# Stick-breaking projections of two heads at a time by seven block products, with the split sets of x stored and reloaded

## The chip, the cores and the metric

The kernel runs on one core of one Trainium2 chip. Its time is device microseconds for one launch. The kernel before takes 2082.61 us, the median of two runs (2079.24 and 2085.99).

The engines are called as the profile calls them: PE is TensorE (matmuls; PEld are its weight loads), DVE is VectorE, ACT is ScalarE, POOL is GpSimd, and SP is the engine that issues nearly all transfers of this kernel.

## The reference

One decoder layer on 1024 tokens of width 2048, in float32:

```python
h = rmsnorm(x, g_pre)
u = h @ w_in                       # 2048 -> 7184 columns, split among the groups
gq, gk, gv, g_gate, g_lr, sq, sk, sv, s_gate = split(u)
log_a = log_sigmoid(g_lr @ w_a2 + b_a) / 16
o_gla = rmsnorm(gla_chunked(gq, gk, gv, log_a), g_gla_head) * silu(g_gate)   # 4 heads
o_sb  = stick_breaking(sq, sk, sv) * silu(s_gate)                            # 8 heads of 128
#   z = q k^T / sqrt(128);  A[t,s] = sigmoid(z_ts) * prod_{s<j<t} (1 - sigmoid(z_tj))
x = x + rmsnorm(concat(o_gla, o_sb) @ w_out, g_post)
x = x + sigmoid(x @ w_g + b_g) * (p @ w_p)
```

## The kernel before, in words

All activations stand transposed: 128 channels in the partitions, tokens along the row. A token half `hf` has 512 tokens. PE multiplies a pair of 128-channel blocks at a time into a PSUM tile of 512 tokens (`dn`, four buffers). To keep float32 precision each operand is split into a rounded high part and the rest, by `split` (lines 112 to 114: a copy on ACT, a subtraction on DVE), and each product is three matmuls: high by high, low by high, high by low (`hi`/`lo` or `wh`/`wl` are weights, `ah`/`al` activations).

**The units.** `dense` (line 144) makes one unit: 128 output columns for both halves, over all 16 channel blocks. It loads the weights in four blocks of 256 KB (`wload`, line 123: two `raw` buffers, four `hi`, four `lo`), and each block feeds 4 channel blocks x 2 halves x 3 matmuls. There are 16 units for GLA (k, q and two of v for each of 4 heads) and 24 for stick-breaking (k, q, v for each of 8 heads). The result is scaled by `rstd`, the norm of x, on its way out of PSUM (`evac_plain`, `evac_turned`, lines 311 to 329); v is turned by a transposing transfer (`turn_by_dma`, line 331: ACT, SP) and copied together by DVE.

**Attention beside the units.** `gla` (line 352) and `sb` (line 541) are generators in the queue `jobs`. After every channel block of a unit `step` (line 174) advances them by `rate[1]` steps, 1.0 for GLA and 0.9 for stick-breaking, and every `pace[1]` steps the queue `beside`. In `sb` a head takes 38 steps: its k is split, then for each of 6 items `scores` (line 580) makes z on PE, two sigmoids on ACT, masks on POOL (memset, affine select), a scan and a product on DVE, and a transposing transfer. After L1 = 8 steps `turned` (line 611) copies the result together on DVE (line 618) and splits it, and after L2 = 8 more `values` multiplies it by the turned v. The queries' factor 1/sqrt(128) is a constant scale of the sigmoids (lines 592 and 593).

**The gate.** The 16 blocks of gate columns come from seven block products per block row (a Strassen-Winograd scheme over 2 x 2 blocks: two halves of channels, two halves of tokens, two halves of columns). `x_sums` (line 690) makes four sums of x's blocks (S1 to S4) on ACT and DVE beside the units, one k in 60 steps, and stores them unsplit. Sixteen of the products are small ones under the last of the attention (`small_product`, line 778: two blocks of 256 KB), the other 40 are wide (`product`, line 899: 512 KB weights, `wr`, `wh`, `wl`). Sums of weights are made by DVE (`add`, `sub`, lines 881 and 884) and stored for later products (`g2_d`, `g3_d`); sets of x are loaded from their stored sums and split again (`x_set`, `fill`).

The output projection and the last gate follow with the same scheme; the change leaves them alone.

**What sets the order.** A planner orders each engine's instructions ahead of the run, by its own costs and by priority: program order, moved ahead by `tc.high_priority(offset=...)`. Each engine then works strictly in that order, and waits where an operand is not there. Buffers of a tag are reused in turn, so a load can wait for the last reader of its buffer.

POOL issues one transfer in the whole kernel (line 108), SP and ACT the others. The scratch of POOL's transfers is set in line 1379:

```python
nc = bacc.Bacc("TRN2", target_bir_lowering=False, num_devices=1,
               dynamic_dma_scratch_size=512)
```

## Time and profile before

| | before |
|---|---|
| median of two runs | 2082.61 us (2079.24 to 2085.99) |
| span of the profiled execution | 2075.1 us |
| PE busy | 2060.6 us (99%), 9712 matmuls |
| PEld busy | 1706.3 us (82%) |
| DVE busy | 1481.9 us (71%) |
| ACT busy | 874.1 us (42%) |
| POOL busy | 112.0 us (5%) |
| moved by DMA | 352.81 MB, mean 170 GB/s |
| granted clock of PE | 1.000 |

The profile is one execution, which has a page and a trace. The page gives its span, from the first to the last instruction, and no other time of that execution; the runs' times include what lies around the span. A group's row reads: line, engine, operation, output<-inputs by the program's names, shape, count | busy us, mean ns of one | idle us of the engine just before them, and what ended it. A row of windows reads: stretch, its length, then for each engine busy us and number of instructions, the granted clock, the mean busy share of the 16 DMA engines, GB/s. A row of waits reads: who <- for whom: us in total, times, longest. A row of transfers has the size and the median us from issue to landing. A matmul's duration overlaps with the next one's, so their means do not add up to time.

### The profile page before, as it was taken

What the parts mean: (1) busy time and instruction counts of PE and PEld (TensorE: products, weight loads), DVE (VectorE), ACT (ScalarE), POOL (GpSimd) and SP (SyncE); (2) the same over time, 40 slices, a digit from 0 to 9 for tenths busy, and PEclk for the clock granted to TensorE, in tenths of its full rate; (3) what the DMA queues carried; (4) which work ended last, traced back from release to release, by engine and by line L of the source; (5) the groups of instructions that cost most, each with busy time, mean ns of one, the idle gap of its engine ahead of it and who ended that gap; (6) DMA issues with size and microseconds to landing.
All of it is one profiled execution on the core that took longest, in us unless ns stands there. A gap on an engine that the chain in (4) does not pass through costs nothing.

```text
span 2075.1 us, 26732 instructions
## 1 busy us (share of the span) xinstructions
PE 2060.6 (99%) x9712; PEld 1706.3 (82%) x9712; DVE 1481.9 (71%) x2243; ACT 874.1 (42%) x1390; POOL 112.0 (5%) x229
## 2 busy tenths in 40 slices
PE   9999999999999999999999999999999999999998
PEld 6788888888888888888888788888888888888887
DVE  8657777676766676666567677788778687886765
ACT  7333334333454554555447423344233334423322
POOL 4100000000011011101001000000000000000000
PEclk9999999999999999999999999999999999999999
DMA  6222222232243344443326798888978486886752
GB/s 219 69 67 78 82 78 82 66 87 67 62 126 88 106 107 108 113 105 97 84 79 156 213 328 295 306 298 303 335 283 269 163 313 229 307 292 210 243 190 98
DMA packets 229700, 352.81 MB, mean 170 GB/s; under 512 B 124336, under 2 KB 129344, under 8 KB 229568
## 3 DMA queue, kind: packets, MB, share of 16 engines
q1 hardware_dynamic: 228960, 349.00, 53.2%
q10 hardware_dynamic: 576, 2.10, 0.3%
q8 instruction: 76, 1.25, 0.2%
q14 instruction: 56, 0.46, 0.1%
q0 software_dynamic: 32, 0.01, 0.0%
HBM read 249.85 MB, written 73.92 MB: 156 GB/s over the span
## 4 chain that ended last, share of the span: by engine, by line
PE 90%; DVE 3%; DMA 3%; issue 2%; ACT 1%; SPq 0%; POOL 0%; DVEq 0%; ACTq 0%; POOLq 0%
PE dn L101 79%; PE z L101 5%; PE t L101 3%; PE o L101 3%; DMA E<-X 1%; DMA xraw<-xT 1%; DVE rstd L235 0%; DMA u<-xT 0%; DVE lo L114 0%; DVE al L252 0%; DVE X L603 0%; DVE E L608 0%; DMA raw<-w_gate 0%; ACT hi L113 0%; ACT ah L251 0%
## 5 line engine op out<-in xcount | busy, mean ns | idle before, releaser
L101 PE MATMUL dn<-ah,hi 128*128 128x512 f32 x1408 | 561.7, 399 | 2.3 <-ACT u L736 1.9
L101 PE MATMUL dn<-ah,lo 128*128 128x512 f32 x1408 | 549.6, 390 | 0.2 <-DVE lo L114 0.2
L101 PE MATMUL dn<-al,hi 128*128 128x512 f32 x1408 | 549.4, 390 | 0.0
L101 PE MATMUL dn<-ah,wl 128*128 128x512 f32 x1216 | 473.4, 389 | 0.0
L101 PE MATMUL dn<-al,wh 128*128 128x512 f32 x1216 | 473.1, 389 | 0.0
L101 PE MATMUL dn<-ah,wh 128*128 128x512 f32 x1216 | 473.1, 389 | 0.0
L101 PEld LDWEIGHTS dn<-ah,hi 128*128 128x128 f32 x1408 | 265.0, 188 | 60.2 <-issue 3.6
L101 PEld LDWEIGHTS dn<-al,hi 128*128 128x128 f32 x1408 | 264.3, 188 | 57.6 <-DVE al L252 0.4
L101 PEld LDWEIGHTS dn<-ah,lo 128*128 128x128 f32 x1408 | 265.2, 188 | 48.1 <-DVE lo L114 0.5
L113 ACT ACTIVATE wh<-wr 128x1024 fp32r<-128x1024 f32 x152 | 159.4, 1055 | 268.1 <-PE dn L101 168.9
L101 PEld LDWEIGHTS dn<-ah,wl 128*128 128x128 f32 x1216 | 228.3, 188 | 48.7 <-DVE wl L114 1.2
L101 PEld LDWEIGHTS dn<-al,wh 128*128 128x128 f32 x1216 | 228.3, 188 | 47.3
L101 PEld LDWEIGHTS dn<-ah,wh 128*128 128x128 f32 x1216 | 228.3, 188 | 47.3
L114 DVE TENSOR_TENSOR wl<-wr,wh 128x1024 fp32r<-128x1024 f32 x152 | 185.0, 1218 | 7.0 <-ACT wh L113 6.7
L113 ACT ACTIVATE hi<-raw 128x512 fp32r<-128x512 f32 x192 | 119.7, 625 | 153.4 <-PE dn L101 137.9
L114 DVE TENSOR_TENSOR lo<-raw,hi 128x512 fp32r<-128x512 f32 x192 | 134.7, 703 | 59.6 <-ACT hi L113 59.5
L333 ACT ACTIVATE X<-E 128x256 uint16<-128x256 uint16 (+2 forms) x96 | 81.0, 844 | 142.8 <-DVE E L608 70.2
L603 DVE TENSOR_TENSOR_SCAN X<-X 128x128 f32<-128x128 f32 (+2 forms) x96 | 97.8, 1019 | 14.4 <-POOL X L597 13.0
L618 DVE COPY v<-E 128x512 uint16<-128x512 uint16 (+1 forms) x160 | 64.1, 430 | 48.5 <-DMA E<-X 45.3
L114 DVE TENSOR_TENSOR s<-v,s 128x512 fp32r<-128x512 f32 (+1 forms) x82 | 52.6, 642 | 61.1 <-ACT s L113 60.9
L884 DVE TENSOR_TENSOR wr<-wr,wr 128x1024 f32<-128x1024 f32 x48 | 58.7, 1223 | 49.4 <-issue 15.1
L881 DVE TENSOR_TENSOR wr<-wr,wr 128x1024 f32<-128x1024 f32 x48 | 58.7, 1224 | 47.5 <-DMA wr<-w_g 34.0
(246 smaller groups left out, 2292.6 us busy)
## 6 DMA issues: line engine op xcount, KB each, us to landing
raw<-w_in SPq DMA_DIRECT2D x160, 256.0 KB, 2.7
wr<-w_g SPq DMA_DIRECT2D x64, 512.0 KB, 4.4
wr<-w_out SPq DMA_DIRECT2D x56, 512.0 KB, 4.8
wr<-w_gate SPq DMA_DIRECT2D x40, 512.0 KB, 5.2
g_d<-wr SPq DMA_DIRECT2D x32, 512.0 KB, 3.8
wr<-g_d SPq DMA_DIRECT2D x32, 512.0 KB, 4.5
ar<-h_d SPq DMA_DIRECT2D x28, 512.0 KB, 4.9
ar<-og_d SPq DMA_DIRECT2D x25, 512.0 KB, 5.3
```

The source lines that it names most:

```text
L101: PE.matmul(o, lhsT, rhs, start=start, stop=stop)
L113: A.activation(hi, src, AF.Copy)
L114: (eng or V).tensor_tensor(lo, src, f(hi), op=ALU.subtract)
L333: A.activation(pl.rearrange("p (two n) -> p two n", two=2), src.bitcast(U16)[:, :2 * n].rearrange("p (n two) -> p two n", two=2), AF.Copy)
L603: V.tensor_tensor_scan(rev, rev, rev, initial=kq[:, n:n + 1], op0=ALU.mult, op1=ALU.bypass)
L618: V.tensor_copy(to[:, :, :m, j], w[:, :, 2 * g:2 * g + m])
L881: V.tensor_tensor(dst, a, b, op=ALU.add)
L884: V.tensor_tensor(dst, a, b, op=ALU.subtract)
```

## The change

**Pairs of heads.** The 24 stick-breaking units become 12 pairs of units: for two heads k beside q of each, and the two v. A pair is a block matrix of 2 (halves of channels) x 2 (columns) by 2 (token halves), made by the seven products that the gate already used, each over 8 channel blocks: 24 matmuls for one token half's sum. `by_waves` makes four of the seven (with the sets A11, s1, S2, A22), `by_stages` three (A12, S4, S3). The pairs go three at a time through first and second passes: pairs 0 to 5 first waves, then stages, pairs 6 to 11 first stages, then waves.

**Sets of x.** `x_sets` replaces `x_sums`: it runs in the GLA units (one k in 25 steps), splits its four sums at once, and stores high and low parts, as also those of the plain blocks A11, A12 and A22. Four sets of 8 high and 8 low tiles are resident at a time; `swap` and `load_set` reload a set over one that is done with, 8 transfers of 512 KB, without splitting again. 8 sets are reloaded in the stick-breaking products and 3 in the gate's. The last GLA unit (`dense_by_blocks`) goes by blocks of 12 matmuls, so that two sets are free early.

**Sums of weights.** Within a chain the next product's weights are the last ones plus another block. `extend` adds that block to the tile in place by a transfer that accumulates, issued by POOL. `onto` does the same with results: a first pass writes k, q and v (unscaled) to DRAM, the second accumulates onto them there.

**The attention** fetches k, q and v from DRAM as it comes to a head (`fetch`, `take`), scales k and v by `rstd` on DVE, and turns v then; q's scale goes into the sigmoids as a column per token (`rq`, made by eight transposes on PE in `norm_first`). It starts when two heads are complete, after 33 of the 84 products, and runs at a rate of 1.0. Half of the copies in `turned` go to ACT (`regroup`).

**The gate** has 32 small products (in batches of 3, 3 and 2 by `by_waves`) and 24 wide ones. The weights' sums on DVE and their storing fall to one addition per column block.

The diff, cut to its core:

```diff
+def pair_offsets():
+    offs = []
+    for h in range(0, SB_HEADS, 2):
+        offs += [(OFF_SK + P * h, OFF_SQ + P * h), (OFF_SK + P * h + P, OFF_SQ + P * h + P),
+                 (OFF_SV + P * h, OFF_SV + P * h + P)]
     return offs
...
-RATE_SB = 0.9
+RATE_SB = 1.0
...
+Q1, V0, V1, NEXT_Q, NEXT_K = 8, 3, 14, 30, 33
...
-LAST_11 = 4
-PACE_QKV, PACE_TAIL = 15, 4
+RATE_TAIL = 1.0
+PACE_X, PACE_SET = 5, 2
+ACCUMULATE, REGROUP = True, 1
+BATCHES = ((0, 1, 2), (3, 4, 5), (6, 7))
...
+        def regroup(j, dst, src):
+            if j >= REGROUP:
+                A.activation(dst, src, AF.Copy)
+            else:
+                V.tensor_copy(dst, src)
...
+            def fetch(h, what, hf):
+                if (h, what, hf) not in fetched and h in sb_ready:
+                    fetched[h, what, hf] = t = at("u")
+                    dma2(t, kqv_d[h][what][hf])
+
+            def take(h, what, hf):
+                fetch(h, what, hf)
+                return fetched.pop((h, what, hf))
...
+                    raw = take(h, 0, hf)
+                    kh[hf], kl[hf] = at(tag, dt=F32R), at("u", dt=F32R)
+                    V.tensor_tensor(raw, raw, rstd[hf], op=ALU.mult)
+                    split(kh[hf], kl[hf], raw)
...
+                    def turn_first():
+                        t = take(h, 2, hf)
+                        V.tensor_tensor(t, t, rstd[hf], op=ALU.mult)
+                        vp[hf] = turn_by_dma(t, HT, "u", "u")
+
+                    def turn_last():
+                        full, w = at("u"), vp[hf]
+                        V.tensor_copy(full.bitcast(U16).rearrange("p (c t two) -> p two c t", c=4, two=2), w)
+                        vp[hf] = at("u", dt=F32R), at("u", dt=F32R)
+                        split(*vp[hf], full)
...
-                    A.activation(kq[:, :n], z[:, :n], AF.Sigmoid, scale=-scale)
-                    A.activation(sg[:, :n], z[:, :n], AF.Sigmoid, scale=scale)
+                    for t, r in ((kq, rq[1]), (sg, rq[0])):
+                        A.activation(t[:, :n], z[:, :n], AF.Sigmoid, scale=r[:, 4 * hf + qi:4 * hf + qi + 1])
...
-                            V.tensor_copy(to[:, :, :m, j], w[:, :, 2 * g:2 * g + m])
+                            regroup(j, to[:, :, :m, j], w[:, :, 2 * g:2 * g + m])
...
+            tp = ps("z")
+            for c in range(4):
+                PE.transpose(ch(tp, c), ch(rstd[hf], c), idn)
+            for t, scale in zip(rq, (1.0, -1.0)):
+                V.tensor_scalar(t[:, 4 * hf:4 * hf + 4], tp[:, ::P], scale * float(P) ** -0.5, None, op0=ALU.mult)
...
             def keep(name, k, t):
-                dma2(part(sx_d[name][k // 2], k), t)
-
+                hi, lo = xs.tile([P, HT], F32R, tag="xh", name=nm("xh"), bufs=2), t.bitcast(F32R)
+                split(hi, lo, t)
+                for d, s in zip(sx_d[name][k // 2], (f(hi), t)):
+                    dma2(part(d, k), s)
...
+                A.activation(a21, a21, AF.Copy, scale=g)
+                V.scalar_tensor_tensor(s1, s1, g8, a21, op0=ALU.mult, op1=ALU.subtract)
+                yield 1
+                V.scalar_tensor_tensor(a21, a11, gminus[:, k:k + 1], a21, op0=ALU.mult, op1=ALU.add)
                 keep("S3", k, a21)
...
+                store_plain()
+                yield 1
+                a12 = x_part(0, k + 8)
+                V.scalar_tensor_tensor(a11, a11, gminus[:, k:k + 1], s1, op0=ALU.mult, op1=ALU.subtract)
+                keep("s1", k, s1)
...
+        def load_set(name, slot):
+            got = []
+            for i, (hf, kp) in enumerate(home[slot]):
+                pair = act_wide(hf, kp)
+                for d, t in zip(sx_d[name][i], pair):
+                    with tc.issue_after(last_load[0]):
+                        dma2(f(t), d)
+                    yield 1
+                got.append(pair)
+            sets[name] = parts(got)
+
+        def swap(old, new):
+            sets.pop(old, None)
+            slot = place.pop(old)
+            place[new] = slot
+            beside.append(load_set(new, slot))
...
+            for hf, q in ((1, 0), (1, 1), (0, 2), (0, 3), (0, 0), (0, 1), (1, 2), (1, 3)):
+                hi, lo = wload(wsrc[q])
+                begin, end = q == (0 if hf else 2), q == (3 if hf else 1)
+                for kk in range(4):
+                    ah, al = acts[hf][4 * q + kk]
+                    sl = slice(kk * P, (kk + 1) * P)
+                    mm(out_ps[hf], hi[:, sl], ah, begin and kk == 0, False)
+                    mm(out_ps[hf], lo[:, sl], ah, False, False)
+                    mm(out_ps[hf], hi[:, sl], al, False, end and kk == 3)
+                    if kk % 2:
+                        step()
+                if (hf, q) == (1, 1):
+                    swap("A21", "s1")
+                if (hf, q) == (0, 3):
+                    swap("A12", "S2")
...
+        def begin(i, src):
+            chain[i] = []
             for q in range(2):
...
+                t = wt("ch", 6)
+                last_load[0] = dma(t, part(src, q)).ins
+                chain[i].append(t)
+
+        def extend(i, src):
+            for q, t in enumerate(chain[i]):
+                if ACCUMULATE:
+                    G.dma_start(t, part(src, q), accum_op=ALU.add)
+                    continue
+                raw = wt("raw", 2)
+                last_load[0] = dma(raw, part(src, q)).ins
+                V.tensor_tensor(t, t, raw, op=ALU.add)
...
+                    hi, lo = wt("hi", 4, F32R), wt("lo", 4, F32R)
+                    split(hi, lo, chain[i][q])
...
+        def onto(dst, t, first):
+            if first:
+                dma2(dst, t)
+            else:
+                G.dma_start(dst, t, accum_op=ALU.add)
+
+        def kept(p, scale=1.0):
+            t = wt("pt", 4)
+            A.activation(t, p, AF.Copy, scale=scale)
+            return t
...
+        def by_waves(items, first, weight, at_d, swaps, mid=None):
+            upper, fifth = {}, {}
+            names = ("A11", "s1", "S2", "A22")
+            blocks = ((0, 0), (0, 1), (1, 1), (1, 0))
+            for s, x in sorted(((s, x) for s in range(4) for x in range(len(items))),
+                               key=lambda v: (1, v[1] + 1.5) if v[0] == 2 else v):
+                i = items[x]
+                if mid and (s, x) == (2, 0):
+                    mid()
+                with early():
+                    (begin if s == 0 else extend)(i, weight(i, *blocks[s]))
+                p = ps("dn")
+                small_product(names[s], i, p)
+                if x == len(items) - 1 and names[s] in swaps:
+                    swap(names[s], swaps[names[s]])
+                with soon():
+                    if s == 0:
+                        upper[i] = kept(p)
+                        onto(at_d("c11", i), upper[i], first)
+                    elif s == 1:
+                        fifth[i] = p
+                    else:
+                        V.tensor_tensor(upper[i], p, upper[i], op=ALU.add)
+                    if s == 2:
+                        t = wt("pt", 4)
+                        V.scalar_tensor_tensor(t, fifth[i], -1.0, upper[i], op0=ALU.mult, op1=ALU.subtract)
+                        for m in ("c12", "c22"):
+                            if at_d(m, i) is not None:
+                                onto(at_d(m, i), t, first)
+                    elif s == 3:
+                        onto(at_d("c21", i), upper[i], first)
+
+        def by_stages(items, first, weight, at_d, swaps):
+            for m in ((2, 3, 7) if first else (3, 7, 2)):
+                name = {2: "A12", 3: "S4", 7: "S3"}[m]
+                for i in items:
+                    with early():
+                        if m == 7:
+                            extend(i, weight(i, 0, 1))
+                        else:
+                            begin(i, weight(i, 1, 1 if m == 3 else 0))
+                    p = ps("dn")
+                    small_product(name, i, p)
+                    with soon():
+                        onto(at_d({2: "c11", 3: "c12", 7: "c22"}[m], i), kept(p), first)
+                        if m == 7:
+                            onto(at_d("c21", i), kept(p, -1.0), first)
...
+        to_2, to_1 = {"A11": "S4", "s1": "S3", "S2": "A12"}, {"A12": "A11", "S4": "s1", "S3": "S2"}
+        def sb_items(stage, first, b, swaps={}):
+            stage(range(3 * b, 3 * b + 3), first, lambda i, kh, nh: w_sb[i, kh, nh], sb_d, swaps)
+            pace[1] = PACE_SET
+            if not first:
+                sb_ready.update({2 * b: True, 2 * b + 1: True})
+                rate[1] = RATE_SB
+
+        sb_items(by_waves, True, 0)
+        sb_items(by_waves, True, 1, to_2)
+        sb_items(by_stages, False, 0)
+        sb_items(by_stages, False, 1)
+        sb_items(by_stages, True, 2)
+        sb_items(by_stages, True, 3, to_1)
+        sb_items(by_waves, False, 2)
+        sb_items(by_waves, False, 3)
...
+        def gate_batch(js, swaps={}, mid=None):
+            by_waves(js, True, lambda j, kh, nh: w_gate[kh, nh, j],
+                     lambda m, j: part(g_d[m][j // 2], j) if m in g_d else None, swaps, mid)
+
+        rate[1] = RATE_TAIL
+        for js in BATCHES[:-1]:
+            gate_batch(js)
...
+    gate_batch(BATCHES[-1], {"A11": "A12", "s1": "S3", "S2": "S4"}, to_wide)
...
+                w2_ = wsplit(wload2(w_gate[1, 0, j]))
+                t3, b22 = wload2(w_gate[0, 1, j]), wload2(w_gate[1, 1, j])
+                add(t3, t3, b22)
+                w7, w3 = wsplit(t3), wsplit(b22)
+                if j % 2 == 0:
+                    with tc.issue_after(last_load[0]):
+                        dma2(st_v[j // 2], g_d["c21"][j // 2])
+                        dma2(st_u[j // 2], g_d["c12"][j // 2])
+            if j % 2 == 0:
+                p11 = staged(g_d["c11"][j // 2])
+            p = product(need("A12"), w2_)
+            gate(j, 0, p, part(p11, j), add)
+            if j == 7:
+                job(fill("A11", 0, plain(og_d[0])))
+                rate[1] = 1.0
+            p = product(need("S3"), w7)
+            gate(j, 1, p, v(j), lambda z, p, c: sub(z, c, p))
+            gate(8 + j, 1, p, u(j), add)
+            p = product(need("S4"), w3)
+            gate(8 + j, 0, p, u(j), add)
...
```

More of the change, by code (lines that the diff above doesn't have):

```diff
@@ L211, in layer @@
     pair = {}
+    x_wide = {}
     acc = {}
@@ L662, in layer @@
         sb_ready = {}
+        kqv_d = [[[dram.tile([P, HT], F32, name=f"kqv{h}{i}{hf}_d") for hf in HALVES] for i in range(3)]
+                 for h in range(SB_HEADS)]
         def norm_first(hf):
@@ L782, in small_product @@
+        def small_product(name, i, p):
+            while name not in sets:
+                assert beside
+                advance(beside)
+            a = sets[name]
+            for q in range(2):
+                with tc.high_priority(offset=700):
+                    hi, lo = wt("hi", 4, F32R), wt("lo", 4, F32R)
+                    split(hi, lo, chain[i][q])
                 for kk in range(4):
@@ L808, in keep_11 @@
-        def keep_11(j, new):
-            def go(p):
-                t = new()
-                V.tensor_tensor(t, p, part(u1_s[j // 2], j) if j < 6 else u1_s[j], op=ALU.add)
-                dma2(part(c11_d[j // 2], j), t)
-            return go
-        while beside:
-            advance(beside)
-        rate[1], pace[1] = RATE_TAIL, PACE_TAIL
-        beside.append(x_set("S2", 1))
-        for j in range(8):
-            small_product(x_act[0][:8], w_gate[0, 0, j], keep_u1(j))
-        while beside:
-            advance(beside)
@@ L858, in state @@
         def state(which):
-            return [act.tile([P, W], F32, tag=f"{which}0_{kp}", name=nm("st")) for kp in range(4, 8)]
+            return [act.tile([P, W], F32, tag=f"{which}{hf}_{kp}", name=nm("st")) for hf, kp in home[0]]
         def to_slot(s, i, raw):
@@ L1023, in finish, with need @@
             dma2(og_d[hf][kp], z)
-        def gates_11():
-            for i in range(4):
-                finish(staged(c11_d[i]), 0, i)
-                yield 1
-        t2_d, t3_d = drams("g2_d", 8), drams("g3_d", 8)
-        dma2(st_u[3], u1_d)
+        def need(name):
+            while name not in sets:
+                assert beside
+                advance(beside)
+            return sets[name]
         for j in range(8):
             with ahead():
-                b11, t1, t2 = (wload2(w_gate[kh, nh, j]) for kh, nh in ((0, 0), (0, 1), (1, 1)))
-                sub(t1, t1, b11)
-                sub(t2, t1, t2)
-                w2, w1 = wsplit(t2), wsplit(t1)
-                add(b11, b11, t2)
-                dma2(t2_d[j], t2)
-                dma2(t3_d[j], b11)
-            p = product(g_sets["S2"], w2)
-            with soon():
-                add(u(j), p, part(u1_s[j // 2], j) if j < 6 else u(j))
-            p = product(g_sets["S1"], w1)
-            with soon():
-                add(v(j), p, u(j))
@@ L1048, in layer @@
-        drain()
-        job(fill("S3", 1, plain(sx_d["S3"])))
-        job(fill("S4", 2, plain(sx_d["S4"])))
-        job(gates_11())
-        for j in range(8):
-            with ahead():
-                t4, t2 = wload2(w_gate[1, 0, j]), wload2(t2_d[j])
-                add(t4, t4, t2)
-                w = wsplit(t4)
-            p = product(x_act[1][8:], w)
-            with soon():
-                add(u(j), p, u(j))
-        drain()
-        for j in range(8):
-            with ahead():
-                w = wsplit(wload2(t3_d[j]))
-            p = product(sets["S3"], w)
-            gate(j, 1, p, u(j))
-            gate(8 + j, 1, p, v(j))
@@ L1069, in layer @@
-        drain()
-        job(fill("A11", 0, plain(og_d[0])))
-        for j in range(8):
-            with ahead():
-                w = wsplit(wload2(w_gate[1, 1, j]))
-            p = product(sets["S4"], w)
-            gate(8 + j, 0, p, v(j))
-        drain()
+                w2_ = wsplit(wload2(w_gate[1, 0, j]))
[3 more added lines that the diff above has]
+                if j % 2 == 0:
+                    with tc.issue_after(last_load[0]):
+                        dma2(st_v[j // 2], g_d["c21"][j // 2])
+                        dma2(st_u[j // 2], g_d["c12"][j // 2])
```

244 lines of the change are left out of this document (121 added, 123 removed).

## The prediction

> **What bounds the kernel now.** First the page's totals, then the stages by windows, then the same windows for the `dn` tiles alone, then who PE waited for.
>
> ```profile
> span 2075.1 us, 26732 instructions
> PE 2060.6 (99%) x9712; PEld 1706.3 (82%) x9712; DVE 1481.9 (71%) x2243; ACT 874.1 (42%) x1390; POOL 112.0 (5%) x229
> PE 90%; DVE 3%; DMA 3%; issue 2%; ACT 1%; SPq 0%; POOL 0%; DVEq 0%; ACTq 0%; POOLq 0%
> ```
> ```profile
> core 0: us, PE busy (x) PEld busy (x) DVE busy (x) ACT busy (x) POOL busy (x), PEclk, DMA share, GB/s
> 75.00:439.00 364.00, 363.50 (x1846) 301.83 (x1845) 256.12 (x501) 135.76 (x230) 13.48 (x13) 1.00 0.26 75
> 439.00:1081.00 642.00, 640.91 (x3159) 539.10 (x3158) 429.73 (x831) 318.01 (x615) 62.22 (x172) 1.00 0.37 96
> 1187.00:1390.00 203.00, 203.00 (x898) 168.07 (x897) 154.98 (x157) 66.97 (x67) 0.00 (x0) 1.00 0.88 306
> ...
> 850.00:900.00 50.00, 50.00 (x247) 42.38 (x246) 31.97 (x63) 25.67 (x52) 6.49 (x19) 1.00 0.41 112
> 1100.00:1150.00 50.00, 50.00 (x243) 42.21 (x242) 39.14 (x75) 34.47 (x70) 7.19 (x19) 1.00 0.63 163
> 1150.00:1200.00 50.00, 47.09 (x218) 38.61 (x217) 31.69 (x47) 19.99 (x33) 0.00 (x0) 1.00 0.77 244
> 1450.00:1500.00 50.00, 50.00 (x222) 41.39 (x222) 39.07 (x37) 15.15 (x16) 0.00 (x0) 1.00 0.92 334
> ```
> ```profile
> 850.00:900.00 50.00, 43.42 (x182) 33.08 (x180) 2.73 (x4) 0.00 (x0) 1.00 0.41 112
> 1200.00:1250.00 50.00, 50.00 (x222) 41.39 (x221) 6.57 (x10) 0.00 (x0) 1.00 0.91 321
> ```
> ```profile
> PE dn L101 <- ACT u L736: 1.9, 1, 1.9
> PE t L101 <- ACT s L113: 1.8, 2, 1.0
> ```
>
> PE is busy for 99% of the span and carries 90% of the chain of waits. A busy PE can hide gaps, so I took two other signs. In a stage of products alone 222 `dn` matmuls fit into 50 us, 0.225 us each, and PEld stays near 42 of 50 in the stages with attention too. And the longest entry among PE's waits is 1.9 us. So time goes down with PE's work as long as nothing starves it. The stages, by the `dn` counts: GLA units to 439 us, stick-breaking units to 1081, small gate products to 1187, wide gate products to 1390, then two stages the change leaves alone. In the second stage PE is full while DVE has 67%, ACT 50% and DMA 37%; in the fourth it is full beside DMA at 88%.
>
> The profiled span lies 7.5 us under the median of the two runs (2082.6) and 4.1 under the faster one. I work on the span and add 7.5.
>
> **Removed from PE.** A unit took 4 blocks x 4 steps x 2 halves x 3 = 96 matmuls, so 24 stick-breaking units took 2304. Now 12 pairs take 7 products of 8 x 3 = 24 matmuls, which is 2016. The gate had 56 products and keeps 56 (32 small, 24 wide). So 288 matmuls go: 288 x 0.226 = 65 us (0.226 lies between the 0.225 above and the 0.2267 of the chain row 344.35 / 1519). Everything is on the path, since PE is the chain there.
>
> ```profile
> 1172.74 344.35 PE dn L101 x1519
> L492 PE MATMUL t<-c,E 128*128 128x128 f32 x32 | 4.9, 274 | 0.3 <-DVE E L390 0.3
> raw<-w_gate SPq DMA_DIRECT2D x32, 256.0 KB, 2.9
> wr<-w_gate SPq DMA_DIRECT2D x40, 512.0 KB, 5.2
> ```
>
> **Added on PE's path.** Eight transposes for the rows of `rq`: 8 x 0.27 = 2.2 us. The change of weight pools after the last GLA unit: a load of 2.9 us and one split (below, 1.3) where it is not covered, 4.2 us, or nothing where the freed tiles come early; I take 4. The draining of the attention ahead of the last four gate products stands in both kernels (PE 47.09 of 50 in the row of 1150), so no term.
>
> **Moved to DVE and ACT.**
>
> ```profile
> L113 ACT ACTIVATE hi<-raw 128x512 fp32r<-128x512 f32 x192 | 119.7, 625 | 153.4 <-PE dn L101 137.9
> L114 DVE TENSOR_TENSOR lo<-raw,hi 128x512 fp32r<-128x512 f32 x192 | 134.7, 703 | 59.6 <-ACT hi L113 59.5
> L315 DVE TENSOR_TENSOR u<-dn,rstd 128x512 f32<-128x512 f32 x38 | 25.5, 684 | 3.6 <-PE dn L101 3.4
> L1088 ACT ACTIVATE st<-dn 128x512 f32<-128x512 f32 x8 | 4.6, 580 | 0.0
> L618 DVE COPY v<-E 128x512 uint16<-128x512 uint16 (+1 forms) x160 | 64.1, 430 | 48.5 <-DMA E<-X 45.3
> L113 ACT ACTIVATE s<-v 128x512 fp32r<-128x512 f32 (+1 forms) x82 | 47.8, 582 | 58.4 <-DVE v L618 32.3 <-PE t L101 20.7 <-DVE eb L607 3.6
> L251 ACT ACTIVATE ah<-xraw,c 128x512 fp32r<-128x512 f32 x32 | 21.8, 712 | 6.3 <-DMA xraw<-xT 3.8 <-DMA c<-g_pre 2.5
> L708 DVE SCALAR_TENSOR_TENSOR u<-u,c,u 128x512 f32<-128x512 f32 x8 | 6.0, 747 | 0.5 <-ACT u L707 0.5
> ```
>
> A split tile now feeds 12 matmuls instead of 24, so the four `hi` and `lo` buffers cover 4 x 12 x 0.226 = 11 us instead of 22, and splits come twice as often. Take the 50 us from 850 on: 182 `dn` matmuls, 1.90 old units or 7.58 new products. Of DVE's 31.97, 7.58 splits are 5.3 and 3.8 evacuations 2.6, and 24.1 are attention; of ACT's 25.67, 4.7 are splits and 20.9 the rest. The attention now gets a step per 6 matmuls (rate 1.0 for 0.9): x1.11, 26.7 and 23.2. New splits: 15.2, so 10.7 on DVE and 9.5 on ACT. Evacuations, per 7 products 3 on DVE and 5 on ACT: 2.2 and 3.1. Scaling k and v by `rstd` after the reload, 0.8 head x 4 tiles: 2.2 on DVE. Half of the L618 copies to ACT: -3.4 on DVE, 8 x 0.58 = +4.7 on ACT. Sigmoids whose scale is now a column: 19 x (0.712 - 0.625) = +1.7 on ACT. DVE gets 38.4 of 50 (77%), ACT 42.2 (84%). The row of 1100 has small products under attention with DVE 39.1 and ACT 34.5 and PE at 50.00: DVE is covered by that row, ACT is beyond it. I take 4 us of PE waits for it, with 0 and 38 as ends (the rival below).
>
> In the GLA units the sums of x are made earlier and split there: 32 x 0.747 + 32 x 0.703 = 46 us on DVE, less some 10 of the old sums that fell there: 256 + 36 = 292 of 364, 80%, against 70%. ACT gets 8 x 0.71 + 32 x 0.625 = 26 more and stays under half. PE's matmuls of the GLA steps are hidden by the same W0 to W2 steps as before; no term, and the same rival holds it. In the gate the weights' sums leave DVE (32 wide additions become 8), which gains nothing: PE 203.00 of 203 hides them already.
>
> **Transfers.** In the stick-breaking products, with 512 KB as 0.524 MB: 36 block loads 18.9 MB, 48 accumulating ones 25.2; 48 results written 12.6 and 48 accumulated 12.6; 48 fetched 12.6; 8 sets of x at 8 x 0.524, 33.6: 78 MB plain and 38 accumulating, where the old stage moved 642 us x 96 GB/s = 62 MB, of which 36 are weights and sums of x. Kept are some 17 for attention, so 132 MB in 577 us: 229 GB/s. The trace ran at 306 to 334 GB/s without a loss on PE, so bandwidth is covered while an accumulating byte costs like a plain one. If its destination is read as well, as it must be, it counts up to twice: 294, still under 306. No term.
>
> The accumulating transfers go out on POOL: 4 x 2 of weights and 4 of results per pair, 144, and 48 in the gate: 192.
>
> ```profile
> L108 POOL DMA_DIRECT2D c<-g_pre x1 | 0.7, 702 | 0.8 <-POOLq L1378 0.8
> L597 POOL TENSOR_SCALAR_AFFINE_SELECT E<-E 128x128 f32<-128x128 f32 x64 | 36.0, 563 | 21.1 <-ACT E L593 20.2
> ```
>
> The only transfer of POOL in the trace took it 0.70 us: 192 x 0.7 = 134 us of an engine that is 95% idle. A product and its attention take 24 x 50 / 182 = 6.6 us, and the masks behind an issue on POOL (affine selects, which the scan waits for) stand in a chain that has 8 steps until its turned result is read. What waits there is an issue for the split that still reads its tile; that split is done up to two products ahead of use, and the next use of the tile is two or three products on: some 13 us for a landing of 2.9 to 5.2. Hidden, so no term; the other end is the last rival.
> [...]
>
> **The sum.** -65 + 2.2 + 4 + 4 = -55: span 2020, time 2028. Without the two fours it is 2020 in time, and a shorter drain (2.9 us) with scatter gives 2010.
>
> **Rivals.**
> *ACT and DVE feed too late.* For it: 84% of ACT, in queues that also wait for transposes, with half the cover. Against: the row of 1100. If the 83 products under attention (51 stick-breaking, 32 gate; 547 us) stretch by 7%, PE waits 38 us instead of 4: 2062.
> *DMA becomes the bound.* It decides when an accumulating byte costs over 2.2 plain ones ((306 x 0.577 - 94) / 38). At 2.6 the stage is 193 plain MB, 630 us at 306 GB/s, 53 us over the 577: 2081. At three it is 103 over: 2131. Against: the sets of x can slip later without harm.
> *POOL's transfers go one at a time* (the slower side). Results are accumulated in the second pass over the pairs. Its wave half has 36 weight and 24 result transfers in 24 products, 158 us less 24 x 0.86 of masks (6.49 per 50): 2.3 us each. Its stage half has 36 in 18 products: 2.9 each. In the first waves it is 4.4, in the gate (48 in 32 products) about 4. If POOL cannot start one until the last has landed, each takes 0.7 + 2.9 = 3.6 us: 60 x 1.3 + 36 x 0.7 = 103 us lost, 2028 + 103 = 2131; with 5.2 us to land (twice the bytes) 5.9 each, and 216 + 109 + 54 + 91 = 470: 2498. It decides from 2.3 us on, and at 3.1 the gain is gone. For it: line 1379 gives such transfers 512 bytes a partition of scratch, and the change leaves that line alone. Against: nothing in the trace, which never had two in flight.
> [...]
>
> **Chances.** From no change a measurement of this kernel tells about 2%: below 2041 is faster, above 2124 slower. Forecast (2010 to 2041) 0.48. Late feeding 0.18, of which 0.04 stay below 2041 and 0.01 pass 2124. DMA 0.08: 0.06 between, 0.02 above. POOL 0.20: 0.02 below, 0.07 between, 0.11 above. Something not named, or matmuls that stay, 0.06: 0.02 between, 0.04 above. Faster 0.48 + 0.04 + 0.02 = 0.54; same 0.13 + 0.06 + 0.07 + 0.02 = 0.28; slower 0.01 + 0.02 + 0.11 + 0.04 = 0.18. The forecast's own range is 2010 to 2041. For 8 in 10 it has to reach into the rivals: to 2100 it takes in the late feeding, DMA's price and the lower third of POOL's, with some 0.17 above and 0.03 below.
>
> **What would show it.** Right: 9432 matmuls on PE (9712 - 288 + 8), `dn` still at 222 per 50 us in products alone, PE 99% busy, and the `dn` rows of `ch` splits with idle time put down to PE. Late feeding: PE waiting for `lo` or `hi` in a span with ACT near 50 of 50. DMA: a share above 0.95 after 440 us with landings of weights far above 5 us. POOL: issues of over 2.3 us a piece, ACT or DVE waiting for `ch`, and the `E` or `X` selects late. The forecast is wrong if PE's busy time falls by 60 us or more and the span by under 35.

## The result, and the profile after

The changed kernel takes 2382.53 us (median of two runs, 2382.33 and 2382.74) against 2082.61 before: 1.144 times as long, interval 1.140 to 1.149. The forecast was 2028.

First the page's totals of the changed kernel, its two main DMA queues (packets, MB, share of the 16 engines' time; q0 holds POOL's transfers) and the chain of waits by engine.

```profile
span 2381.0 us, 27312 instructions
PE 2103.3 (88%) x9432; PEld 1700.1 (71%) x9432; DVE 1491.2 (63%) x2264; ACT 997.0 (42%) x1622; POOL 270.9 (11%) x421
q1 hardware_dynamic: 250992, 405.64, 52.7%
q0 software_dynamic: 27680, 50.35, 14.4%
PE 22%; DMA 6%; DVE 5%; issue 5%; ACT 1%; POOL 1%; SPq 0%; POOLq 0%; DVEq 0%; ACTq 0%
```

The 9432 matmuls are there, 280 fewer than before, as forecast. But PE's busy time is 43 us longer, with fewer matmuls. The last line doesn't compare with the 90% of before: its shares add up to 40%, for the chain could be followed back from the end only to some 1430 us, and it doesn't reach the stretch that matters.

The windows tell where: in a stage of products alone PE is full, in the stretch of the stick-breaking products it is not, and its granted clock (the column after POOL) falls there.

```profile
core 0: us, PE busy (x) PEld busy (x) DVE busy (x) ACT busy (x) POOL busy (x), PEclk, DMA share, GB/s
700.00:800.00 100.00, 61.88 (x241) 48.86 (x239) 26.40 (x49) 31.35 (x62) 22.71 (x37) 0.81 0.61 114
1100.00:1200.00 100.00, 62.28 (x248) 48.93 (x249) 42.98 (x78) 38.02 (x72) 24.15 (x43) 0.80 0.63 112
1600.00:1700.00 100.00, 100.00 (x443) 82.80 (x442) 73.29 (x75) 35.45 (x36) 0.00 (x0) 1.00 0.79 273
```

No engine and not DMA is full in 700 to 800 or 1100 to 1200. So engines wait for one another, one after the next. Whom POOL waited for (total, times, longest):

```profile
POOL ch L891 <- issue: 241.6, 61, 8.9
POOL ch L891 <- DVE lo L122: 153.4, 28, 33.5
POOL kqv_d L922 <- issue: 92.2, 24, 6.0
```

"issue" is idle time ahead of an instruction that waits for nothing the profile shows: 241.6 + 92.2 = 334 us ahead of the accumulating transfers (`extend` is line 891, `onto` line 922). POOL's timeline shows its form (start, duration, instruction, idle time before):

```profile
674.34 0.86 POOL L891 DMA_DIRECT2D ch<-w_sb  x1 [3.68 <-issue]
678.52 0.89 POOL L891 DMA_DIRECT2D ch<-w_sb  x1 [3.31 <-issue]
682.70 0.89 POOL L922 DMA_DIRECT2D kqv_d<-pt  x1 [3.29 <-issue]
687.33 0.90 POOL L891 DMA_DIRECT2D ch<-w_sb  x1 [3.74 <-issue]
691.90 0.89 POOL L922 DMA_DIRECT2D kqv_d<-pt  x1 [3.68 <-issue]
696.18 0.90 POOL L922 DMA_DIRECT2D kqv_d<-pt  x1 [3.39 <-issue]
```

One transfer starts every 4.2 to 4.6 us, 4.4 in the mean, whichever buffers it uses. The table of DMA issues suggests the reason, by the median from issue to landing:

```profile
ch<-w_sb POOLq DMA_DIRECT2D x96, 256.0 KB, 4.2
ch<-w_sb SPq DMA_DIRECT2D x72, 256.0 KB, 3.4
```

An issue every 4.4 us, a landing in 4.2: by these rows one transfer is in flight at a time. Behind POOL's queue wait the masks, behind those the scan on DVE, and behind that PE, for the tiles of the scores `z`:

```profile
DVE X L657 <- POOL X L651: 143.2, 46, 22.7
```
```profile
PE z L109 <- DVE st L122: 58.2, 22, 14.3
PE z L109 <- ACT E L647: 52.4, 11, 13.9
PE z L109 <- ACT st L121: 47.8, 7, 22.5
```

Before, PE's longest wait was 1.9 us; now it is 22.5. All of PE's waits add up to 270 us in the whole table, against 8 before: 183 ahead of `z` (the attention) and 68 ahead of `dn` (the products).

### The profile page after: what moved, and what is told of

It reads as the page before. It is cut to its first block, busy times and chain, and to the rows that moved or that the text cites. A ratio compares the mean times of both kernels' runs of the same rounds, so it can differ in the third digit from the quotient of the medians.

```text
span 2381.0 us, 27312 instructions
## 1 busy us (share of the span) xinstructions
PE 2103.3 (88%) x9432; PEld 1700.1 (71%) x9432; DVE 1491.2 (63%) x2264; ACT 997.0 (42%) x1622; POOL 270.9 (11%) x421
## 3 DMA queue, kind: packets, MB, share of 16 engines
q1 hardware_dynamic: 250992, 405.64, 52.7%
q0 software_dynamic: 27680, 50.35, 14.4%
## 5 line engine op out<-in xcount | busy, mean ns | idle before, releaser
L109 PE MATMUL dn<-ah,hi 128*128 128x512 f32 x1440 | 598.7, 416 | 33.8 <-ACT hi L121 19.6
L109 PE MATMUL dn<-ah,lo 128*128 128x512 f32 x1440 | 587.6, 408 | 19.6 <-DVE lo L122 16.2
L109 PE MATMUL dn<-al,hi 128*128 128x512 f32 x1440 | 582.4, 404 | 0.0
L109 PE MATMUL dn<-al,wh 128*128 128x512 f32 x1088 | 425.0, 391 | 9.3 <-DMA al<-S33l_d 4.9
L109 PE MATMUL dn<-ah,wh 128*128 128x512 f32 x1088 | 426.3, 392 | 3.5 <-ACT ah L121 2.7
L109 PE MATMUL dn<-ah,wl 128*128 128x512 f32 x1088 | 426.0, 392 | 2.2 <-DVE wl L122 2.1
L122 DVE TENSOR_TENSOR lo<-ch,hi 128x512 fp32r<-128x512 f32 x232 | 160.2, 694 | 190.2 <-ACT hi L121 185.0
L121 ACT ACTIVATE hi<-ch 128x512 fp32r<-128x512 f32 x232 | 142.9, 621 | 163.6 <-DMA ch<-w_sb 97.2
L109 PE MATMUL z<-b,st 128*128 128x512 f32 (+3 forms) x128 | 53.6, 421 | 121.2 <-ACT E L647 52.4
L891 POOL DMA_DIRECT2D ch<-w_sb x96 | 85.9, 895 | 421.1 <-issue 168.4
```

What stands on the lines that cost most here:

```text
L109: PE.matmul(o, lhsT, rhs, start=start, stop=stop)
L121: A.activation(hi, src, AF.Copy)
L122: (eng or V).tensor_tensor(lo, src, f(hi), op=ALU.subtract)
L891: G.dma_start(t, part(src, q), accum_op=ALU.add)
```

## Experiments

Where only one run was made, differences under some 8 us mean nothing: the kernel before, run beside them, came out between 2079 and 2087.

### Room for more of POOL's transfers

The one number of line 1540 was changed, first to 768 bytes, then to 1024 (there a mask's tile is 128 elements shorter and a gap is left out, to make the room), then to 576.

```diff
-                   dynamic_dma_scratch_size=512)
+                   dynamic_dma_scratch_size=768)
```

> One number is changed: the scratch of POOL's transfers is 768 bytes a partition instead of 512; the order of instructions on every engine stays. Theory (the accumulating transfers go one at a time because the scratch holds only one of them): two fit now, POOL's waits put down to issue fall from 334 us to under 80, and the time from 2382 to 2040-2120. Rival A (POOL's transfers are serial by nature: each waits until the last has landed, whatever the scratch): still 4.2 us from one to the next and 2380. Rival B (POOL's pace is a symptom; ACT and DVE feed PE too late by themselves): the issue waits go, the time stays above 2200.

> Scratch of 1024 bytes, room for it from the unused end of the mask tile and one gap of 128 bytes. Theory: three fit, or more; 2030-2080, and no later than with 768. Rival A: 2380. Rival B: above 2200.

> The changed kernel with 576 bytes of scratch a partition in place of 512; nothing else. [...]

Measured: 768 bytes 2207.9 us (four runs, 1.061 times before, interval 1.059 to 1.064); 1024 bytes 2211.6 (1.063, 1.061 to 1.066); 576 bytes 2219.4 (one run). POOL's waits with 768 bytes:

```profile
POOL ch L891 <- DVE lo L122: 276.3, 71, 33.6
POOL ch L891 <- issue: 49.8, 21, 5.8
```

and its timeline with 576:

```profile
677.42 0.88 POOL L891 DMA_DIRECT2D ch<-w_sb  x1 [4.67 <-DVE st L122]
678.52 0.90 POOL L922 DMA_DIRECT2D kqv_d<-pt  x1 [0.21 <-issue]
683.16 1.79 POOL L891 DMA_DIRECT2D ch<-w_sb  x2 [3.75 <-issue]
```

Two are in flight now: a second issue 1.1 us after the first, then 3.75 us of waiting. 64 bytes of scratch, and nothing else, are worth 163 us; another 192 bytes bring 12 more at most, another 256 none. So by these timelines 576 bytes hold two of these transfers, where 512 hold one (one start every 4.4 us).

The two larger sizes missed their forecast times all the same. The waits put down to issue fell from 334 to 70 us with 768 bytes, as the theory had it, but the time stayed 88 us above the end of its range (2040 to 2120), at what rival B had named, "above 2200". The room was the largest cost, and not the only one.

The path by which the missing room reached PE shows in PE's waits with 768 bytes. The longest rows ahead of `z` are now these:

```profile
PE z L109 <- DVE st L122: 26.2, 22, 3.5
PE z L109 <- ACT E L647: 16.1, 11, 4.4
```

All waits ahead of `z` fell from 183 to 60 us, while those ahead of `dn` hardly changed (68 and 65). So by these rows the loss of the one-at-a-time transfers came to PE by way of the attention, not by weights that were late for the products.

### How much of it is accumulation

Then POOL's transfers were taken away in steps. First with 512 bytes and the weights' second blocks still sent by POOL, but not accumulated (the weights' sums are left out).

```diff
-                    G.dma_start(t, part(src, q), accum_op=ALU.add)
+                    G.dma_start(t, part(src, q))
```

> Scratch 512 as in the changed kernel; the 144 transfers of weights still go out on POOL but overwrite instead of accumulating, so the sums of weights are left out and the products are those of single blocks. The 48 accumulations of results stay. Theory, in the form that an accumulating transfer takes twice the room because it reads its destination too: the plain ones fit two or three at a time, their issue waits (242 us) nearly go, those of the results (92 us) stay, 2080-2180. Rival A: 4.2 us apart as before, 2350-2380. If only the bytes count, the landing is faster (3 for 4.2 us) but still one at a time: 2250-2300.

Measured: 2180.4 us. A row of the page, and one of POOL's waits:

```profile
q0 software_dynamic: 18464, 50.35, 10.1%
```
```profile
POOL kqv_d L922 <- issue: 47.0, 14, 6.3
```

This is the upper end of the theory's range. In the changed kernel 27680 packets less the 32 of the kernel before, over 192 transfers, are 144: 9 per DMA engine. Here 48 transfers still accumulate (6912), and the other 144 have 11520: 80 each, 5 per engine. So a plain transfer that POOL issues has about half the packets of an accumulating one of the same tile. POOL's waits for room fell from 334 to 80 us with it (32.5 of them ahead of `ch`), and its issue takes 0.56 us in the mean where the accumulating one takes 0.89. The timeline also has a plain issue 2.3 us behind an accumulating one (at 625.70 and 623.44), where the accumulating ones land in 4.5 us in the median, so by these figures a plain one still fits beside it into 512 bytes.

Next, all 192 as plain transfers of SP (weights' sums and the accumulation of results left out):

```diff
-                    G.dma_start(t, part(src, q), accum_op=ALU.add)
+                    last_load[0] = dma(t, part(src, q)).ins
-                G.dma_start(dst, t, accum_op=ALU.add)
+                dma2(dst, t)
```

> No accumulating transfer at all: weights and results go by plain transfers on SP that overwrite, so the sums of weights and the second pass onto the results are left out; everything else of the change stays (products, sets of x, splits, attention). Theory: the rest of the change gives what the sum of the prediction said, 2020-2060, with PE at 98% or more. Rival B: PE waits for ACT or DVE, above 2100.

Measured: 2115.1 us, as rival B had it (above 2100), and not the 2020 to 2060 of the theory. SP's plain transfers of these tiles have 9 packets per engine as well:

```profile
q1 hardware_dynamic: 278640, 455.98, 66.8%
```

That is 27648 packets more than q1 has in the changed kernel, or 144 for each of the 192. So the number of packets alone doesn't make the price of accumulating.

With 768 bytes, only one of the two kinds accumulates (the other's sums left out):

> 768 bytes of scratch; only the weights' second blocks come by POOL's accumulating transfers (144 of the 192), the products' results are all stored by plain transfers of SP (their sums are left out). The question is which half of the accumulating transfers holds the 93 us between 768 bytes (2208) and no transfer on POOL (2115). Theory A, the weights' sums do it (a split waits for the landing of two transfers in a row, and POOL waits in order for the split that frees the tile): 2190 us (2175 to 2205). Theory B, the results do it (they take half of POOL's queue in the second pass and fill DMA): 2135 us (2120 to 2150). In equal parts: 2160.

> 768 bytes of scratch; only the results of the second pass are accumulated by POOL's transfers (48), the weights' second blocks come by plain transfers of SP (their sums are left out). Theory A, the weights' sums hold the 93 us: 2130 us (2115 to 2145). Theory B, the results hold them: 2185 us (2170 to 2205). In equal parts: 2160.

Measured: weights alone 2174.4, results alone 2149.7. Over 2115 that is 59 and 35 us, together 94, where both together cost 93: the two add up, the weights hold the larger part, and both times lie between theory A and equal parts. And 768 bytes with the masks left out:

```diff
-                        G.memset(kq[:, n:n + 1], 1.0)
+                        V.memset(kq[:, n:n + 1], 1.0)
-                        for t, fill in ((kq, 1.0), (sg, 0.0)):
-                            G.affine_select(...)
```

> 768 bytes of scratch, and the triangular masks of the attention left out (the 64 selects on POOL are gone, and the 32 fills of a column stand on DVE), so POOL has transfers alone in that stretch. Theory A, the 93 us that 768 bytes leave over the kernel without POOL's transfers are masks queued behind transfers that wait for their tile: 2130 us (2115 to 2150). Theory B, they are the time that sums take by way of a transfer (the split of the sum waits for the landing, the tile is free again late, and an accumulating packet takes twice the time of a plain one): 2195 us (2175 to 2210), since DVE waits only 24.5 us for masks with 768 bytes.

Measured: 2192.5, theory B: once two transfers fit, masks queued behind transfers cost about 15 us, not 93. What the 59 is made of was not separated. The accumulating itself, the landing that a split waits for (with 768 bytes a `ch` transfer lands in 4.8 us, where SP's plain ones take 3.2 without it), and the order in which POOL takes its transfers, since many of them wait for the split that frees their tile (the 276 us for `lo` above), may each have a part in it.

### The weights' sums on DVE

The other branch of `extend`: the second block comes by a plain transfer of SP, DVE adds it; three high and three low buffers in place of four make the room. The results still accumulate. First with 512 bytes, then with 768.

```diff
-ACCUMULATE, REGROUP = True, 1
+ACCUMULATE, REGROUP = False, 1
-                    hi, lo = wt("hi", 4, F32R), wt("lo", 4, F32R)
+                    hi, lo = wt("hi", 3, F32R), wt("lo", 3, F32R)
```

> The changed kernel (512 bytes of scratch) with the weights' sums made as the code's other branch has it: the second block comes by a plain transfer of SP into a tile of its own and DVE adds it; three high and three low buffers in place of four make the room. The products' results still go into DRAM by POOL's accumulating transfers. Theory A, the loss over the kernel without POOL's transfers lies in sums by way of POOL's transfers: 192 additions of 0.65 to 0.7 us are some 130 us of DVE, which is 60 to 73% busy there, so most of it is hidden: 2145 us (2120 to 2175), better than 768 bytes. Theory B, DVE is full then (88% and more of the attention's stretch) and feeds later still: 2210 us or more.

> The change whole, with two repairs: 768 bytes of scratch, and the weights' sums added by DVE behind plain transfers (three high and three low buffers). Theory: the 512 bytes cost 76 us of POOL's waiting for room behind the results there, of which at most 25 reached the end; so 2160 us (2150 to 2175), still slower than before by 3 to 4%. Rival: the waits for the splits of the DVE sums (63 us of PE's waits) are the path, and the time stays at 2183 (2175 to 2190).

Measured: 2183.3 (1.048, 1.045 to 1.052) and 2161.8 (1.038, 1.034 to 1.042). With 512 bytes the results still stood in POOL's queue, and PE waited for the splits:

```profile
POOL kqv_d L922 <- issue: 76.2, 17, 6.8
```
```profile
PE dn L109 <- ACT hi L121: 33.0, 14, 11.1
PE dn L109 <- DVE lo L122: 30.4, 40, 4.7
```

The first time lies between its two theories. DVE had 144 additions more and 85 us more of busy time, not the 192 and 130 of the expectation. The second time is what its expectation said. With 768 bytes this is the fastest whole version of the change that was run, and it is 3.8% slower than the kernel before.

### What is left without POOL: 87 us over the forecast

The kernel with no transfer on POOL still takes 2115, not 2028. Two runs take the sets of x away from it: one without building, storing and loading them (every product reads what its slot held first), one that builds and stores them and only loads none again.

```diff
-                beside.append(x_sets())
+                pass
...
-                pair = act_wide(hf, kp)
-                for d, t in zip(sx_d[name][i], pair):
-                    with tc.issue_after(last_load[0]):
-                        dma2(f(t), d)
+                pair = x_wide[hf, kp]
+                for t in pair:
                     yield 1
```

The second run has the second part only.

> The kernel with every accumulating transfer made a plain one of SP (sums left out), and besides without the split sets of x: none are built or stored, and none are loaded again; every product reads the tiles that its slot held first. Theory A, the 87 us by which that kernel was over my forecast are the sets' work and traffic (DVE and ACT splits in the first 500 us, reloads that wait for their slots): 2060 us (2040 to 2075). Theory B, they are attention's steps on ACT and DVE that come late beside fewer matmuls: 2100 us (2090 to 2115), because only some 14 us that the first 600 us lose can go.

> No transfers on POOL, and the split sets of x are built, split and stored as in the change, but no set is loaded again (the products read what their slot held first). All the sets' work was worth 46 us (2115 to 2069). Theory A, most of it is the building in the GLA units (DVE 46 us more, 33 MB of stores): 2100 us (2095 to 2108). Theory B, most of it are the reloads, which come late for the first product of a set and fill DMA beside the results: 2082 us (2075 to 2090).

Measured: 2069.1 and 2086.5. All of the sets are worth 46 us, the reloads 29 of them (nearer theory B), the building 17. The building shows in the first 500 us, first in the kernel with it (no reloads) and then in the one without:

```profile
0.00:500.00 500.00, 482.70 (x2396) 389.25 (x2397) 377.64 (x698) 228.39 (x391) 44.74 (x36) 0.99 0.49 157
```
```profile
0.00:500.00 500.00, 494.03 (x2474) 402.00 (x2475) 350.44 (x655) 209.82 (x359) 41.97 (x36) 1.00 0.29 85
```

With the building PE has 11 us and 78 matmuls less in that stretch, although DVE is busy for only 76% of it.

Of the 41 us that remain, four runs on the kernel without sets asked for the place. The first leaves the attention out (its steps only copy a tile per head and half to its result), the second gives it the old rate, the third and fourth take the copies of `regroup` off ACT, to DVE as before, or to POOL.

```diff
-        jobs.append(sb())
+        jobs.append(sb_stores())
```
```diff
-RATE_SB = 1.0
+RATE_SB = 0.9
```
```diff
-ACCUMULATE, REGROUP = True, 1
+ACCUMULATE, REGROUP = True, 2
```
```diff
-                A.activation(dst, src, AF.Copy)
+                G.tensor_copy(dst, src)
```

> Without sets and without transfers on POOL, and with the stick-breaking attention left out: its steps only copy one tile per head and half into its result. By the counts of my forecast the 83 products beside it are 1992 matmuls, 450 of 547 us, so 97 us of PE work go. Theory A, products alone are fed in time although a split tile serves 12 matmuls in place of 24, and the 41 us need the attention beside them: 2069 - 97 - 41 = 1931 us (1915 to 1945), and PE is busy 99% and more of 700 to 1100. Theory B, the halved cover of the splits is late by itself: 1965 us (1950 to 1975), and PE is under 97% there.

> Without sets and without transfers on POOL, and the attention's rate beside the stick-breaking products back from 1.0 step to the 0.9 of the kernel before. Theory A, the 41 us left over my forecast come from the attention being dense beside fewer products: PE's idle time falls in proportion to the rate's excess and the time is 2058 us (2050 to 2064), as long as the attention still ends before its drain. Theory B, density is not it (the waits stand in the order of one attention step, however far apart): 2068 us (2065 to 2075); later than that if the attention no longer ends ahead of the wide products and PE waits for its drain.

> Without sets and without transfers on POOL, and with one part of the change undone: both copies that regroup the turned weights of the attention are on DVE again (REGROUP 2), none on ACT. ACT loses some 35 us of work in the 400 us from 750 on, where it is 65 to 76% busy, DVE gains some 24 and goes from 71 to 77%. Theory A, ACT is what feeds the scores late: 2055 us (2045 to 2063). Theory B, the chain between the two engines is late, whichever of them does the copy, or DVE is the later one: 2070 us or more (2065 to 2085).

> Without sets and without transfers on POOL, and the half of the regrouping copies that the change put on ACT is done by POOL, which is 6% busy there; DVE keeps its half. ACT loses some 35 us in the 400 us from 750 on and DVE gains nothing (with the copies on DVE the time was 2064). Theory A, the load of ACT and DVE together is what feeds the scores late: 2050 us (2040 to 2058). Theory B, it is the order of the steps, each waiting for the one before on another engine, or the copy on POOL is slow and its masks come late behind it: 2064 us or more.

Measured: 1910.0 without the attention, 2068.9 with the old rate, 2064.5 with the copies on DVE, 2067.1 with them on POOL. The windows without attention, and then those of the kernel with it (no sets in both):

```profile
700.00:800.00 100.00, 100.00 (x443) 82.86 (x442) 25.19 (x37) 34.54 (x60) 0.00 (x0) 1.00 0.54 178
900.00:1000.00 100.00, 100.00 (x443) 82.86 (x442) 42.51 (x60) 27.55 (x43) 0.00 (x0) 1.00 0.60 206
```
```profile
700.00:800.00 100.00, 93.11 (x445) 76.15 (x445) 66.81 (x120) 76.07 (x143) 11.49 (x30) 1.00 0.68 179
800.00:900.00 100.00, 91.36 (x437) 74.78 (x436) 67.04 (x121) 73.63 (x143) 12.90 (x36) 0.99 0.67 177
```

Products alone are fed without a gap though a split tile serves 12 matmuls: 443 in 100 us, as in any stage of products. So the loss needs the attention beside them. Leaving it out took off 159 us, where 97 of PE work and 41 of loss were expected. The two pages divide it: the attention's 768 matmuls (9432 less 8664) are 130 us of PE's busy time (2018.5 less 1888.9), more than the 97, and PE's idle time fell by 29 us (from 48.8 to 19.3; 14.5 in the kernel before). So the attention makes PE wait some 30 us; the time without it came out below theory A's range because its own work had been put too low. The other three came out nearest theory B: the old rate changed nothing, and the copies on DVE or on POOL took off 5 and 2 us, which is within the scatter. Neither density nor the load of ACT accounts for the loss. In the kernel without sets, PE's longest waits are for the query's split in the chain of a score, and the weights' splits hardly count:

```profile
PE z L109 <- DVE st L122: 11.4, 12, 2.9
PE z L109 <- ACT st L121: 5.7, 6, 1.9
...
PE dn L109 <- DVE lo L122: 0.2, 1, 0.2
PE dn L109 <- ACT hi L121: 0.2, 1, 0.2
```

Of 41 us of PE's waits there, 28 stand ahead of `z`. That the order of the steps between ACT and DVE makes them is the explanation that is left; it was not shown by a run of its own.

## Why the prediction was wrong, point by point

**The step that failed** is "Hidden, so no term", on the 192 accumulating transfers. It priced them at 0.7 us of POOL each and let them overlap. They go one at a time, every 4.4 us, and even with room for two they cost 93 us over a kernel without them. The last rival had the mechanism and the line, and two of its three signs are there: the selects late for DVE (143 us) and ACT waiting for `ch` (126 us). The third, issues of over 2.3 us a piece, is not there in that form: an issue takes 0.9 us, and the rest is idle time ahead of it. With 4.4 us each its own working gives 60 x (4.4 - 2.3) + 36 x (4.4 - 2.9) + 48 x (4.4 - 4) = 126 + 54 + 19 = 199 us, and room for a second transfer took 163 to 175 off. It got a chance of 0.20, although the prediction found nothing in the trace against it; a resource that the change uses for the first time, with its size in the source, deserved more than that.

How much of the scratch such a transfer takes, no row of before showed. The runs show one accumulating transfer at a time with 512 bytes (4.4 us from one to the next) and two with 576 (a second issue 1.1 us after the first).

**PE's work** fell as forecast in matmuls: 9432, and 222 per 50 us where products stand alone. Its busy time did not fall by the 63 us that the sum has for PE (65 less 2.2). Without POOL's transfers and without sets it is 2018 us, 42 less than before, at a mean clock of 0.994. So the matmuls are gone, and a third of what they should have saved is spent again in PE's own busy time, part of it on the clock.

**The late feeding** had 4 us, with 0 and 38 as ends. Without sets 41 us are left over the forecast. By the spans it is 47 (2067.3 against 2020): 27 of PE's idle time and 20 of its busy time. The shares were forecast too high (ACT 84%, DVE 77%; without sets both are at 67 to 76% in the quoted windows) and the loss too low: an engine 70% busy was still late for the steps that PE waited for. The halved cover of the splits, which the rival named, is not the cause: without attention the products are fed without a gap, and with it PE waits 0.4 us for the weights' splits. So where the rival came near in size, its mechanism did not hold.

**The sets of x** had no term, in the GLA units ("hidden by the same W0 to W2 steps") and as transfers ("bandwidth is covered"). They cost 17 and 29 us.

**DMA.** q0 took 14.4% of the engines' time for 50.35 MB and q1 52.7% for 405.64: 0.286 and 0.130 a MB, so an accumulating byte took 2.2 times the engine time of the mean plain one, near the "up to twice" of the prediction and just where its rival decides. Against the same tiles sent plain by POOL (10.1% of 2178.7 us, less the 48 that still accumulate) it is some 1.9 by the same working. DMA's share is 0.61 and 0.63 in the two starved windows, so it is not the bound there. Part of the 59 and 35 us may be that price.

**POOL's issue** was put at 0.7 us from a 0.70 us row and measured 0.89:

```profile
L891 POOL DMA_DIRECT2D ch<-w_sb x96 | 85.9, 895 | 421.1 <-issue 168.4 <-DVE lo L122 107.0 <-DVE v L556 12.8
```

The issues took 38 us more in all than 192 x 0.7. With 768 bytes they took as long, 0.89 us in the mean, and 264 of the 334 us of idle time ahead of them went. So the length of an issue is not what made the loss.

**The sum in runs.** 2028 forecast, + 41 left without sets, + 17 building sets, + 29 loading them, + 59 accumulating weights, + 35 accumulating results, + 175 one transfer at a time (163 of them by 64 bytes): 2384, against 2382.5. The terms are steps from one run to the next and the 41 is what is left, so they must nearly meet. What they do show is that the two kinds of accumulating transfer add up, and how large each step is.

Two smaller points. The 7.5 us added to the span were mostly scatter, since the changed kernel's span lies 1.5 us under its time. And the prediction said that it would be wrong if PE's busy time fell by 60 us and the span did not follow; PE's busy time did not even fall, which has to do with the clock, below.

## What to carry to other kernels

When a change gives an engine a new kind of transfer, ask how many of them its scratch has room for before asking what they move: here 64 bytes of scratch were worth 163 us, and the sign of a full scratch was idle time put down to "issue" ahead of one transfer after another, which together with the issue lasted about one landing (4.4 us against 4.2). Expect more of an accumulating transfer than of a plain one: here it took 1.9 to 2.2 times the time on DMA, and more of the scratch (in the same 512 bytes POOL's waits put down to issue ahead of `ch` were 242 us, and 32.5 with plain ones). And look at what feeds PE before counting work taken off it as a gain: here a mean busy share of 70% on ACT and DVE did not show that they were in time.

## What was not expected of the hardware

PE's clock fell in its long gaps (to 0.50 in the two below), and such a gap was paid for twice. Three neighbouring stretches of the changed kernel's trace, idle, busy, idle, and then two pieces of the busy one:

```profile
726.40:736.40 10.00, 0.00 (x0) 0.00 (x0) 1.21 (x2) 1.18 (x3) 1.77 (x2) 0.50 0.54 109
736.60:753.50 16.90, 12.52 (x44) 10.00 (x44) 3.57 (x7) 6.37 (x14) 3.52 (x4) 0.80 0.40 61
753.70:763.70 10.00, 0.14 (x1) 0.14 (x1) 2.15 (x5) 1.57 (x2) 2.11 (x4) 0.50 0.58 106
...
738.60:740.60 2.00, 2.00 (x7) 1.54 (x6) 1.80 (x3) 1.15 (x3) 0.88 (x1) 0.50 0.45 25
744.60:746.60 2.00, 2.00 (x11) 1.65 (x10) 0.00 (x0) 0.05 (x1) 0.00 (x0) 1.00 0.79 122
```

In each of the two stretches of 10 us in which PE is idle, but for one matmul, the granted clock is 0.50. It stays there for the first 6 us of the work between them, with 7 matmuls in 2 us, is 0.91 in the next 2 us, and only then 1.00, with 11. The same 9432 matmuls were 2103 us of busy time in the changed kernel (mean clock 0.946), 2034 without POOL's transfers (0.985) and 2018 without sets as well (0.994): up to 85 us that no row of waits names.

POOL's small operations also read longer when transfers stood beside them. The fills of one column, before and after:

```profile
L595 POOL MEMSET X<- 128x1 f32 x64 | 7.6, 119 | 294.3 <-DVE E L608 194.5 <-DMA E<-X 48.5 <-ACT st L113 46.8
```
```profile
L649 POOL MEMSET X<- 128x1 f32 x64 | 23.1, 362 | 55.3 <-DVE E L662 55.3
```

119 ns each became 362, and without POOL's transfers (2115 us) they read 117 again, so it goes with the transfers. But in the timeline a fill overlaps the issue ahead of it (one of 0.45 us starts at 624.53, within an issue of 0.88 us from 623.99), so this may be the record of an overlap; the runs don't tell.
